# First weight sums of the second feed-forward made ahead in the first output stage, with a reordered opening, convolution statistics and last gate

## The chip, the cores and the metric

The kernel runs on one core of a Trainium2 chip. The metric is device time in microseconds (us). The engines are PE (TensorE, matmuls and transposes), DVE (VectorE), ACT (ScalarE), POOL (GpSimd) and SP (SyncE, which only issues transfers). Each has a queue of its own and works through it in order; an instruction at its head that waits holds up what is queued behind it.

## The reference

One encoder layer over 1024 tokens of width 1024, in float32, with three residual sub-layers, cut to its core:

```
x = post_norm(x, mod0, 0.5, h -> (silu(h@w1[:, :2816]) * (h@w1[:, 2816:])) @ w1_out)
x = post_norm(x, mod1, 1.0, h -> concat(conformer_conv(h), diff_attention(h)) @ mix_w_out)
x = post_norm(x, mod2, 0.5, h -> (silu(h@w2[:, :2816]) * (h@w2[:, 2816:])) @ w2_out)
post_norm(x, (shift, scale, gate), w, f) =
    layer_norm(2**0.25 * x + w * (1 + gate) * f(x * (1 + scale) + shift)) * g + b
mod = (silu(c) @ w_ada + b_ada), nine rows of 1024
```

## The kernel before, in words

**Stages.** In order of time: the opening, which makes shift and scale of the first sub-layer; the first feed-forward's input phase (to about 495 us); its output stage (to 711); the mixer's projections and convolution (to about 900); attention (to 1125); the mixer's output product (to 1224); the start of the second feed-forward, here called the middle (to about 1300); its input phase (to 1660) and its output stage (to the end).

**Products.** The feed-forward matrices are multiplied by a scheme of seven block products in place of eight, so sums of blocks of weights (`sf`, `S1` to `S4`) and of activations (`r_kt`, `T1` to `T4`) are made first. Every float32 operand is then split into a high part (a copy on ACT, names that end in h) and a low part (a subtraction on DVE or POOL, names in l), and each block product is three matmuls: high by high, high by low, low by high. In the input phase a step j handles 128 gate and 128 up columns; `ra_j`, `rb_j` (or `r_j`, `r4`) are its raw weights, `ah`/`al` the split gate blocks, `sh`/`sl` the split sums, `fi_j` its results in PSUM. In the output stage 77 steps (`prep`, then 12 matmuls `fo`) run over seven products n and 11 blocks k; `prep` runs four steps ahead (`AHEAD`) and makes `gl` and `wr`. `evac` empties the products.

**Opening.** For each of four column blocks kk, `first_mod` forms a row-vector product: DVE sums six of eight weight rows into `ada0a`, PE adds up over partitions (`ada0p`) and does the other two rows itself (`ada0q`); ACT then makes the columns A and B and from them `h`, whose split is `r_kkbh`, `r_kkbl`.

**Attention.** While heads are worked on, the convolution's channel statistics run as side work: `conv_stat(half)` makes `cv` and `cr` on POOL, waits `ST` = 5 turns of the loop and makes `cnm` on DVE. POOL also does the differential subtraction `p`, which is 2.4 us each.

**Middle.** The string `MSEQ` is an order written by hand: tokens for the last pieces of the mixer's output (m, d), the transposes of the normalised x (f, F), the splits and sums of activations (r, s, t, u, v, b), gate splits (G), the weight sums of j = 0 and 1 (X, x, Y, y), raw weights and sums of j = 2 (W) and product steps (p). The letters V and G behind a token name DVE or POOL. An exclamation mark lets the token be issued only behind the last PE piece.

**Last gate.** `ada_gate` makes the last sub-layer's gate row in two halves: eight weight rows are loaded in four pieces `adaw` of 512 KB and summed on DVE (`ada`, L155 and L157), then PE and DVE finish it.

Spill and weight transfers go over SP's queue, the output pieces `gd`, `mwo`, `spill` and `mwi` over POOL's.

Of the kernel before, what the change touches and what calls it, by code (L numbers as in the profile page):

```python
# [38 lines left out]
MSEQ = "m5 G0 f0 r0V f1 d5 r1G !m6 f2 r2V f3 d6 r3G m7 d7 F0 !X0GV x0V | !Y0VG p01 p02 s0GV y0V F2 G1 t0V F1 s1VV t1G s2VV p11 !F3 !X1GV s3VV b0 t2V t3V u0GV b1 v0V u1GG v1V b2 b3 !p12 Y1GG u3VV u2GV v2V v3V x1V !p06 y1G p05 !p16 !p07 p15 !p03 !p17 p04 W0 p13 !p14"  # L39
# [11 lines left out]
def layer_kernel(ctx, tc, a, out):  # L51
# [483 lines left out]
    def out_phase(s, wp, w_out, gd, gate, xs, done, after):  # L535
# [13 lines left out]
        def prep(n, k):  # L549
# [144 lines left out]
    mwi = [dram.tile([D, 2, H], F32, name=f"mwi{g}", tag="mwi", bufs=3) for g in range(3)]  # L694
    mwo = [dram.tile([P, 2, 2, H], F32, name=f"mwo{j}", tag="mwo", bufs=8) for j in range(8)]
    with pool("p1a") as wp:
# [464 lines left out]
    with pool("mattn") as wp:  # L1161
# [81 lines left out]
        def conv_stat(half):  # L1243
# [70 lines left out]
    with pool("p3a") as wp:  # L1314
# [70 lines left out]
        def token(st, tok, n3):  # L1385
# [29 lines left out]
            elif c in "XY":  # L1415
# [141 lines left out]
```

## Time and profile before

| | |
|---|---|
| Runs | 1895.30, 1894.91, 1892.62 us; median 1894.91 |
| Profiled execution | 1899.15 us, its span 1897.4 us |
| Mean granted TensorE clock | 0.99 of full speed |
| PE busy | 1826.3 us |
| DVE busy | 1439.1 us |
| ACT busy | 784.9 us |
| POOL busy | 317.4 us |

The profiled execution lies 4.24 us above the median of the runs. Its time is 1.75 us above its span. Busy time of a matmul includes its drain, so back-to-back matmuls of 128x512 that are shown at 0.39 us start 0.2275 us apart; at half the clock the same ones are shown at 0.63 us.

### The profile page before, as it was taken

To read this page: it belongs to the slowest core of one execution; us is meant where nothing else is said; L and a number is where in the kernel's file an instruction comes from. 1 tells how busy PE (TensorE), PEld (TensorE's weight loads), DVE (VectorE), ACT (ScalarE), POOL (GpSimd) and SP (SyncE) were. 2 spreads that over 40 slices of the span, in tenths; PEclk is the share of its full clock that TensorE was granted. 3 is DMA by queue.
4 is the path that set the end of the run, shared out by engine and by line. 5 is a ranking of instruction groups with operands and counts; after the bars stand their busy time and mean duration, and the time that the engine had idled before them with its cause. 6 is when DMAs were issued, how large, how long until landed. Compare 5 with 4: busy or idle time off the path is not lost. (4 is left out here: it accounts for less than half of the span.)

```text
span 1897.4 us, 23451 instructions
## 1 busy us (share of the span) xinstructions
PE 1826.3 (96%) x8570; PEld 1513.1 (80%) x8570; DVE 1439.1 (76%) x1979; ACT 784.9 (41%) x1292; POOL 317.4 (17%) x322
## 2 busy tenths in 40 slices
PE   5999999999999999999999899979999999999997
PEld 5787888887888887887888788758887888888885
DVE  4988877897688777999676566587776665469888
ACT  2643333333445543122277781453332333354540
POOL 0001111011200011036467540350000000000011
PEclk9999999999999999999999999989999999999999
DMA  9268867785894323222000134125554433187432
GB/s 319 72 225 281 257 228 239 242 268 189 301 322 131 100 60 134 83 95 70 20 1 1 45 134 134 78 83 183 167 166 152 145 120 106 45 293 275 135 113 72
DMA packets 219378, 288.73 MB, mean 152 GB/s; under 512 B 15978, under 2 KB 126687, under 8 KB 219262
## 3 DMA queue, kind: packets, MB, share of 16 engines
q1 hardware_dynamic: 204842, 245.25, 39.9%
q0 software_dynamic: 11072, 38.80, 5.6%
q10 hardware_dynamic: 3348, 3.18, 0.5%
q8 instruction: 67, 1.10, 0.2%
q14 instruction: 49, 0.40, 0.1%
HBM read 209.06 MB, written 78.12 MB: 151 GB/s over the span
## 5 line engine op out<-in xcount | busy, mean ns | idle before, releaser
L587 PE MATMUL fo<-wr,gl 128*128 128x512 f32 x1848 | 421.5, 390 | 1.0 <-DVE pv L630 1.0
L587 PEld LDWEIGHTS fo<-wr,gl 128*128 128x128 f32 x1848 | 346.3, 188 | 74.1 <-DVE pv L630 1.4
L1000 DVE SCALAR_TENSOR_TENSOR cacc<-u,convw,cacc 128x1012 f32<-128x1012 f32 (+14 forms) x120 | 150.9, 1322 | 0.2
L144 DVE TENSOR_TENSOR gl<-gr,gl 128x512 fp32r<-128x512 f32 x148 | 101.4, 691 | 12.5 <-ACT gl L143 11.0
L143 ACT CAST gl<-gr 128x512 fp32r<-128x512 f32 x148 | 90.8, 618 | 26.3 <-DMA gr<-gd 19.4
L144 DVE TENSOR_TENSOR sl<-sf,sh 128x1024 fp32r<-128x1024 f32 x43 | 54.5, 1267 | 59.0 <-ACT sh L143 58.9
L1131 DVE TENSOR_REDUCE mx<-sc 128x1 f32<-128x1024 f32 x64 | 75.5, 1215 | 26.2 <-PE sc L1129 26.0
L219 POOL TENSOR_TENSOR rr<-rv,mhalf 128x1 f32<-128x1 f32 x24 | 22.2, 925 | 431.4 <-DVE rv L217 431.4
L157 DVE SCALAR_TENSOR_TENSOR ada<-adaw,c_act,ada 128x512 f32<-128x512 f32 x98 | 73.2, 747 | 25.3 <-DMA adaw<-in_w_ada_dram 24.8
L143 ACT CAST sh<-sf 128x1024 fp32r<-128x1024 f32 x44 | 46.4, 1054 | 104.8 <-PE fi_16S L373 5.8
L1133 ACT ACTIVATE p<-sc,mx 128x1024 f32<-128x1024 f32 x64 | 71.4, 1117 | 36.1 <-DVE mx L1131 36.0
L395 POOL DMA_DIRECT2D gd<-gf x8 | 4.4, 546 | 413.6 <-DVE gf L461 412.5
L423 ACT ACTIVATE gf<-gf 128x512 f32<-128x512 f32 x44 | 27.8, 632 | 106.0 <-DVE gf L422 103.0
L143 ACT CAST wr<-wa 128x512 fp32r<-128x512 f32 x66 | 41.2, 624 | 71.1 <-PE fo L587 70.1
L443 ACT ACTIVATE gf<-gf 128x512 f32<-128x512 f32 x44 | 27.7, 629 | 98.8 <-DVE gf L442 98.8
L981 PE MATMUL glu<-hm,gluh 128*128 128x512 f32 x256 | 65.6, 392 | 0.0
L1182 POOL TENSOR_TENSOR p<-p,p 128x1024 f32<-128x1024 f32 x27 | 64.2, 2377 | 1.5
L143 ACT CAST wr<-wb 128x512 fp32r<-128x512 f32 x66 | 40.2, 621 | 57.5 <-PE fo L587 40.4
L144 DVE TENSOR_TENSOR wr<-wa,wr 128x512 fp32r<-128x512 f32 x66 | 45.4, 687 | 24.0 <-ACT wr L143 23.7
L1199 PE MATMUL av<-vf,aT 128*128 128x128 f32 x512 | 62.4, 276 | 1.0 <-ACT cacc L1262 1.0
L144 DVE TENSOR_TENSOR sl<-r,sh 128x1024 fp32r<-128x1024 f32 x44 | 53.6, 1221 | 11.8 <-ACT sh L143 11.7
L1199 PEld LDWEIGHTS av<-vf,aT 128*128 128x128 f32 x512 | 59.7, 192 | 1.5 <-ACT cacc L1262 1.3
(3436 smaller groups left out, 4874.1 us busy)
## 6 DMA issues: line engine op xcount, KB each, us to landing
gr<-gd SPq DMA_DIRECT2D x148, 256.0 KB
adaw<-in_w_ada_dram SPq DMA_DIRECT2D x56, 512.0 KB
gd<-gf SPq DMA_DIRECT2D x102, 256.0 KB
r<-in_ffn_w_in_dram SPq DMA_DIRECT2D x84, 256.0 KB
ra<-in_ffn_w_in_dram SPq DMA_DIRECT2D x66, 256.0 KB
mwi<-mw POOLq DMA_DIRECT2D x24, 512.0 KB, 5.9
wb<-in_ffn_w_out_dram SPq DMA_DIRECT2D x44, 256.0 KB
wa<-in_ffn_w_out_dram SPq DMA_DIRECT2D x44, 256.0 KB
```

What stands on the lines that cost most here:

```text
L143: a = S.copy(hi, x)
L144: b = eng.tensor_tensor(lo, x, hi.bitcast(F32), ALU.subtract)
L157: V.scalar_tensor_tensor(acc, raw[:, jj], c_act[:, n : n + 1], acc, ALU.mult, ALU.add)
L423: S.activation(c0, c0, AF.Silu)
L443: pace["S"] = S.activation(c1, c1, AF.Silu).ins
L587: PE.matmul(ps, lhsT=g[:, x, ts_], rhs=w[:, y], start=n in (1, 2, 3) and k == i == 0, stop=k == NK - 1 and i == 2, skip_group_check=n not ...
L981: PE.matmul(q[2 * m + h], lhsT=w[:, m * P : (m + 1) * P], rhs=hm[k][h][:, x], start=k == 0 and n == 0, stop=k == KD - 1 and n == 2,)
L1000: V.scalar_tensor_tensor(acc[:, lo_t:hi_t], u[:, lo_t + sh : hi_t + sh], convw[:, i, jj : jj + 1], acc[:, lo_t:hi_t], ALU.mult, ALU.add,)
L1131: V.tensor_reduce(mx_, ps, axis=AX.X, op=ALU.max, negate=True)
L1133: S.activation(pe, ps, AF.Exp, bias=mx_, accum_out=sm[:, e : e + 1])
L1182: last = G.tensor_tensor(p0, p0, p1, ALU.add)
L1199: PE.matmul(ps[:, 0:P], lhsT=aT[:, kt], rhs=vf[kt][:, h * P : (h + 1) * P], start=kt == 0, stop=kt == 7)
```

## The change

Five places change.

1. **Opening.** DVE sums seven of the eight weight rows and PE one (`NV` now counts rows). The high split `r_kbh` is put right behind `h` of the same block and the next block's columns are ordered behind it (`rounded`); the gate split of j = 0 and its weight sums are put at blocks 0, 1 and 3.
2. **First output stage.** During steps 0 to 71 the sums S1 to S4 of the second feed-forward's weights of j = 0 and j = 1 are made, in eight pieces (a piece is one of two j by one of four k). Every nine steps POOL's queue loads a piece (`sums_load`), and six steps later DVE and ACT make its four sums with their split (`sums_part`), which POOL's queue stores to two new DRAM tiles `mws`.
3. **Attention.** `conv_stat` waits 10 turns in place of 5.
4. **Middle.** The tokens X, x, Y, y are gone; S and T load the ready sums by eight SP transfers of 512 KB. r1, r3 and t1 change from G to V.
5. **Last gate.** `ada_gate` has a staged form: two pieces are loaded and four rows summed, one step later the other two, then the rest, driven from `hook2` at j = 10 to 17; the second half begins at 14 in place of 13.

```diff
-MSEQ = "m5 G0 f0 r0V f1 d5 r1G !m6 f2 r2V f3 d6 r3G m7 d7 F0 !X0GV x0V | !Y0VG p01 p02 s0GV y0V F2 G1 t0V F1 s1VV t1G s2VV p11 !F3 !X1GV s3VV b0 t2V t3V u0GV b1 v0V u1GG v1V b2 b3 !p12 Y1GG u3VV u2GV v2V v3V x1V !p06 y1G p05 !p16 !p07 p15 !p03 !p17 p04 W0 p13 !p14"
+MSEQ = "m5 G0 f0 r0V f1 d5 r1V !m6 f2 r2V f3 S0 d6 r3V m7 d7 F0 | p01 p02 s0VV F2 G1 t0V F1 s1VV t1V s2VV p11 !F3 T0 S1 s3VV b0 t2V t3V u0GV b1 v0V u1GG v1V b2 b3 !p12 u3VV u2GV v2V v3V !p06 p05 T1 !p16 !p07 p15 !p03 !p17 p04 W0 p13 !p14"
-NV = (3, 3, 3, 3)
+NV = (7, 7, 7, 7)
...
+            with tc.issue_after(pace["Y"]):
+                fetch(0)
+                fetch(1)
+            yield
+            for n in (0, 2):
+                with tc.issue_after(pace["V"]):
+                    for q in (n, n + 1):
+                        ada_acc([raws[q]], acc, 2 * q)
+                if n == 0:
+                    with tc.issue_after(pace["Y"]):
+                        fetch(2)
+                        fetch(3)
+                    yield
+            yield
+            rest(acc)
...
+        w2 = a["ffn2_w_in"][0].rearrange("(k e p) (s n) -> k e p s n", e=2, p=P, s=2)
+
+        def sums_load(j, k):
+
+            t = wp.tile([P, 2, 4, P], F32, tag="ms", bufs=1, name=f"ms{j}{k}")
+            for e in range(2):
+                G.dma_start(t[:, 0, 1:3] if e else t[:, 0, 0::3], w2[k, e][:, :, j * P : (j + 1) * P])
+            return t
+
+        def sums_part(t, j, k):
+
+            r = t[:, 0]
+            with tc.issue_after(pace["V"]), tc.issue_after(pace["S"]):
+                V.tensor_tensor(r[:, 2], r[:, 3], r[:, 2], ALU.add)
+                V.tensor_tensor(r[:, 3], r[:, 0], r[:, 3], ALU.subtract)
+                V.tensor_tensor(r[:, 0], r[:, 2], r[:, 0], ALU.subtract)
+                V.tensor_tensor(r[:, 1], r[:, 1], r[:, 0], ALU.subtract)
+                S.copy(t[:, 1].bitcast(F32R), r)
+                V.tensor_tensor(r.bitcast(F32R), r, t[:, 1], ALU.subtract)
+            for x in range(2):
+                G.dma_start(mws[j][:, x, :, k], t[:, x])
...
+            if s == 0 and i < 72:
+                if i % 9 == 2:
+                    ms = sums_load(i // 36, i // 9 % 4)
+                elif i % 9 == 8:
+                    sums_part(ms, i // 36, i // 9 % 4)
...
-            for j in range(2 * n):
+            for j in range(n):
...
-                with tc.issue_after(columns) if kk else nullcontext():
+                with ExitStack() as es:
+                    if kk:
+                        es.enter_context(tc.issue_after(columns))
+                        es.enter_context(tc.issue_after(rounded))
                     summed, columns = first_mod(kk, ada[kk], NV[kk])
                     hb.append(first_h(kk, xb[kk], 0))
+                    hi.append(slot(f"r0_{kk}bh"))
+                    rounded = S.copy(hi[kk], hb[kk]).ins
                 with tc.issue_after(summed):
                     if kk:
-                        right_first(f"r0_{kk - 1}", ops, hb[kk - 1])
-                    if kk == 1:
+                        right_lo(kk - 1)
+                    if kk == 0:
                         L[0].update(in_gate(wp, s, 0, raws[0]))
-                    if kk == 3:
-                        right_first("r0_3", ops, hb[3])
-                        in_sums(wp, s, 0, raws[0], L[0])
+                    elif kk == 1:
+                        in_sums(wp, s, 0, raws[0], L[0], order=(0,))
+                    elif kk == 3:
+                        right_lo(3)
+                        in_sums(wp, s, 0, raws[0], L[0], order=(1,))
...
-            for _ in range(ST):
+            for _ in range(2 * ST):
                 yield
...
+            elif c in "ST":
+                i = int(c == "T")
+                parts = []
+                for x, tag in ((1, "sh"), (0, "sl")):
+                    parts.append(wp.tile([P, 2, 4, P], F32R, tag=tag, bufs=3, name=f"{tag}2_{k}_{i}"))
+                    SY.dma_start(parts[-1].bitcast(F32), mws[k][:, x, i::2])
...
-            if j in (10, 13):
+            if j in (10, 14):
...
-            if j in todo2:
-                todo2.pop(j)()
+            if 10 <= j <= 17:
+                next(todo2["gate"], None)
```

Three places show what the orders become. The first is DVE's queue in the opening, from the second block's split on; `ada0a` are the row sums (x2 counts two in a row), `al_0` the low part of j = 0's gate blocks, `r_kbl` the low part of block k of h. Before:

```order
L729 TENSOR_SCALAR ada0a_317<-ada_1_0_219,c_act 128x512
L731 SCALAR_TENSOR_TENSOR ada0a_317<-ada_1_0_219,c_act,ada0a_317 128x512
L731 SCALAR_TENSOR_TENSOR ada0a_317<-ada_1_1_222,c_act,ada0a_317 128x512 x2
L731 SCALAR_TENSOR_TENSOR ada0a_317<-ada_1_2_225,c_act,ada0a_317 128x512 x2
L144 TENSOR_TENSOR al_0_363<-r_0_200,ah_0_362 128x1536
L144 TENSOR_TENSOR r_0bl<-h_0_0_313,r_0bh 128x1024
L729 TENSOR_SCALAR ada0a_367<-ada_2_0_233,c_act 128x512
L731 SCALAR_TENSOR_TENSOR ada0a_367<-ada_2_0_233,c_act,ada0a_367 128x512
L731 SCALAR_TENSOR_TENSOR ada0a_367<-ada_2_1_236,c_act,ada0a_367 128x512 x2
L731 SCALAR_TENSOR_TENSOR ada0a_367<-ada_2_2_239,c_act,ada0a_367 128x512 x2
L144 TENSOR_TENSOR r_1bl<-h_1_0_355,r_1bh 128x1024
L729 TENSOR_SCALAR ada0a_413<-ada_3_0_247,c_act 128x512
```

After:

```order
L144 TENSOR_TENSOR al_0_318<-r_0_202,ah_0_317 128x1536
L782 TENSOR_SCALAR ada0a_322<-ada_1_0_221,c_act 128x512
L784 SCALAR_TENSOR_TENSOR ada0a_322<-ada_1_0_221,c_act,ada0a_322 128x512
L784 SCALAR_TENSOR_TENSOR ada0a_322<-ada_1_1_224,c_act,ada0a_322 128x512 x2
L784 SCALAR_TENSOR_TENSOR ada0a_322<-ada_1_2_227,c_act,ada0a_322 128x512 x2
L784 SCALAR_TENSOR_TENSOR ada0a_322<-ada_1_3_230,c_act,ada0a_322 128x512
L366 TENSOR_TENSOR r_0_202<-r_0_202 128x512
L367 TENSOR_TENSOR r_0_202<-r_0_202 128x512
L368 TENSOR_TENSOR r_0_202<-r_0_202 128x512
L834 TENSOR_TENSOR r_0bl<-h_0_0_312,r_0bh 128x1024
L144 TENSOR_TENSOR sl_0_0_368<-r_0_202,sh_0_0_367 128x1024
L782 TENSOR_SCALAR ada0a_372<-ada_2_0_235,c_act 128x512
```

The gate's low part stands ahead of the second block's sums, three weight sums and `sl_0_0` stand between the second and third blocks, and each block has one more row.

The second place is POOL's queue in the middle, where the last two tiles of the mixer's output are normalised; `rr_k` is the reciprocal deviation of tile k, `spill_k` its store, `sf_2` the sums of j = 2. Before:

```order
L144 TENSOR_TENSOR r_1bl<-h_10279,r_1bh 128x1024
L1420 TENSOR_TENSOR sf_0_0_10434<-rb_0_9871,ra_0_9870 128x512
L219 TENSOR_TENSOR rr_6_10371<-rv_6_10369,mhalf 128x1
L1327 DMA spill_6_9660<-x_6_9697 128x1024
L144 TENSOR_TENSOR r_3bl<-h_10352,r_3bh 128x1024
L219 TENSOR_TENSOR rr_7_10416<-rv_7_10414,mhalf 128x1
L1424 TENSOR_TENSOR sf_0_1_10518<-ra_0_9870,sf_0_0_10434 128x512
L1327 DMA spill_7_9661<-x_7_9699 128x1024
L1403 TENSOR_TENSOR r_0t_10552<-h_10422,h_10263 128x512
L1420 TENSOR_TENSOR sf_1_0_10629<-rb_1_9877,ra_1_9876 128x512
L1409 TENSOR_TENSOR h_10422<-h_10422 128x512
L1409 TENSOR_TENSOR h_10579<-h_10579 128x512
```

After:

```order
L244 TENSOR_TENSOR rr_5_10376<-rv_5_10374,mhalf 128x1
L1394 DMA spill_5_9737<-x_5_9773 128x1024
L373 TENSOR_TENSOR sf_2_0_10893<-rb_2_10884,ra_2_10883 128x512
L375 TENSOR_TENSOR sf_2_1_10894<-ra_2_10883,rb_2_10884 128x512
L374 TENSOR_TENSOR sf_2_0_10893<-sf_2_0_10893,ra_2_10883 128x512
L244 TENSOR_TENSOR rr_6_10453<-rv_6_10451,mhalf 128x1
L376 TENSOR_TENSOR sf_2_1_10894<-ra_2_10883,sf_2_0_10893 128x512
L1394 DMA spill_6_9738<-x_6_9775 128x1024
L244 TENSOR_TENSOR rr_7_10498<-rv_7_10496,mhalf 128x1
L1394 DMA spill_7_9739<-x_7_9777 128x1024
L1476 TENSOR_TENSOR h_10504<-h_10504 128x512
L1476 TENSOR_TENSOR h_10647<-h_10647 128x512
```

POOL loses the splits `r_1bl`, `r_3bl`, `r_1t1l`, and the sums of j = 0 and 1; the sums of j = 2 stand ahead of and behind `rr_6`.

The third place is DVE's queue in attention at the second half's statistics; `mx` are the row maxima of the scores. Before:

```order
L1237 BN_STATS cst_9092<-cT_9087 128x6
L1238 BN_AGGR cmv_8871<-cst_9092 128x2
L1252 SCALAR_TENSOR_TENSOR cnm_9232<-cmv_8871,cr_9167 128x4
L1131 TENSOR_REDUCE mx_9127<-sc_9122 128x1
L1131 TENSOR_REDUCE mx_9136<-sc_9131 128x1
L1191 COPY aT_9140<-aT_9147 128x512
```

After:

```order
L1304 BN_STATS cst_9160<-cT_9155 128x6
L1305 BN_AGGR cmv_8949<-cst_9160 128x2
L1198 TENSOR_REDUCE mx_9195<-sc_9190 128x1
L1198 TENSOR_REDUCE mx_9204<-sc_9199 128x1
L1319 SCALAR_TENSOR_TENSOR cnm_9416<-cmv_8949,cr_9308 128x4
L1258 COPY aT_9208<-aT_9215 128x512
```

`cnm` stands behind the two maxima; the first half's `cnm` keeps its place.

## Rows read from the trace of the kernel before

**Rows 1.** The page's first part: busy time, share and instructions of each engine.

```profile
PE 1826.3 (96%) x8570; PEld 1513.1 (80%) x8570; DVE 1439.1 (76%) x1979; ACT 784.9 (41%) x1292; POOL 317.4 (17%) x322
```

**Rows 2.** Windows by stage: busy us (instructions) of PE, PEld, DVE, ACT, POOL; clock; DMA.

```profile
0.00:100.00 100.00, 75.48 (x332) 63.84 (x333) 68.03 (x90) 47.64 (x85) 2.01 (x9) 1.00 0.65 198
...
495.00:711.00 216.00, 215.85 (x968) 178.12 (x967) 176.03 (x294) 107.78 (x178) 16.84 (x21) 1.00 0.54 176
...
1224.00:1300.00 76.00, 63.45 (x257) 48.72 (x257) 64.98 (x65) 38.01 (x49) 30.26 (x19) 0.89 0.34 111
```

**Rows 3.** Timeline of DVE in the opening: start, us, instruction, idle before.

```profile
32.04 1.23 DVE L144 TENSOR_TENSOR r_0bl<-h,r_0bh 128x1024 fp32r<-128x1024 f32 x1 [7.36 <-ACT r_0bh L143]
...
42.64 1.23 DVE L144 TENSOR_TENSOR r_1bl<-h,r_1bh 128x1024 fp32r<-128x1024 f32 x1 [5.04 <-ACT r_1bh L143]
...
44.30 3.90 DVE L731 SCALAR_TENSOR_TENSOR ada0a<-ada,c_act,ada0a 128x512 f32<-128x512 f32 x5
...
57.78 1.29 DVE L811 TENSOR_TENSOR t<-h,h 128x512 f32<-128x512 f32 x2
```

**Rows 4.** Waits of PE, 0 to 100 us: total, times, longest.

```profile
PE ada0q L737 <- DMA ada<-in_w_ada_dram: 12.1, 2, 10.3
PE ada0p L747 <- DVE ada0a L731: 6.1, 2, 3.5
```

**Rows 5.** First output stage: DVE and PE timeline, one window, ACT's waits to 600.

```profile
574.13 0.67 DVE L144 TENSOR_TENSOR wr<-wa,wr 128x512 fp32r<-128x512 f32 x1
496.42 179.89 PE L587 MATMUL fo<-wr,gl 128*128 128x512 f32 x792
555.00:565.00 10.00, 10.00 (x46) 8.29 (x45) 10.00 (x17) 3.81 (x7) 0.00 (x0) 1.00 0.91 290
ACT wr L143 <- PE fo L587: 31.1, 21, 1.6
```

**Rows 6.** Attention around the second half's statistics: timelines of POOL and PE, DVE's wait.

```profile
1082.63 2.38 POOL L1182 TENSOR_TENSOR p<-p,p 128x1024 f32<-128x1024 f32 x1
1085.38 1.02 POOL L1248 TENSOR_TENSOR cr<-cv,mhalf 128x4 f32<-128x4 f32 x1
DVE cnm L1252 <- POOL cr L1248: 8.7, 2, 4.4
1089.52 0.71 PE L1113 MATMUL qTl<-ident_r,ql 128*128 128x128 f32 x4 [2.49 <-DVE aT L1191]
```

**Rows 7.** Windows in attention, the middle and behind the gate, columns as above.

```profile
1090.00:1100.00 10.00, 10.00 (x62) 8.89 (x62) 6.28 (x9) 9.18 (x22) 6.75 (x4) 0.85 0.05 16
...
1250.00:1260.00 10.00, 5.15 (x14) 3.05 (x13) 10.00 (x8) 3.15 (x4) 6.34 (x4) 0.67 0.37 105
...
1440.00:1450.00 10.00, 10.00 (x37) 8.08 (x38) 8.81 (x12) 2.70 (x3) 0.00 (x0) 0.83 0.49 167
```

**Rows 8.** Timelines of PE, DVE and POOL in the middle.

```profile
1229.14 0.50 PE L373 MATMUL fi_0A<-r_3bl,ah 128*128 128x512 f32 x1 [1.93 <-POOL r_3bl L144]
1240.19 1.09 PE L1335 MATMUL hT<-ident,x 128*128 128x128 f32 x8 [0.61 <-ACT h L255]
1245.88 2.83 DVE L1403 TENSOR_TENSOR r_2t<-h,h 128x512 f32<-128x512 f32 x1
1244.89 3.27 POOL L144 TENSOR_TENSOR r_1t1l<-r_1t,r_1t1h 128x1024 fp32r<-128x1024 f32 x1
1248.21 0.50 PE L373 MATMUL fi_0A<-r_1t1l,sh 128*128 128x512 f32 x1 [2.85 <-POOL r_1t1l L144]
1287.59 0.39 PE L373 MATMUL fi_2A<-r_0bh,ah 128*128 128x512 f32 x1
```

**Rows 9.** DMA traffic from 1215 to 1262 in 40 slices.

```profile
GB/s 164 282 0 0 0 0 0 0 251 195 0 0 0 0 0 47 275 349 330 303 49 0 0 0 7 0 0 0 0 0 91 133 231 304 134 0 0 0 0 0
```

**Rows 10.** The gate's first half: DVE timeline, and PE's wait, 1420 to 1470.

```profile
1433.78 1.54 DVE L157 SCALAR_TENSOR_TENSOR ada<-adaw,c_act,ada 128x512 f32<-128x512 f32 x2 [3.52 <-DMA adaw<-in_w_ada_dram]
PE fi_9A L373 <- DVE p L439: 2.4, 1, 2.4
```

More of the change, by code (lines that the diff above doesn't have):

```diff
@@ L2 @@
-from contextlib import nullcontext
+from contextlib import ExitStack
 import concourse.bass as bass
@@ L148, in layer_kernel, with ada_acc @@
     w_ada = a["w_ada"][0].rearrange("(p j) n -> p j n", j=KD)
-    def ada_acc(raws, acc):
-        n = 0
+    def ada_acc(raws, acc, n=0):
         for raw in raws:
@@ L185, in ada_cols, with ada_gate, slow, fetch @@
         return rest
-    def ada_gate(wp, take, s, w, g, half):
+    def ada_gate(wp, take, s, w, g, half, staged=False):
         if half == 0:
             SY.dma_start(g, a["b_ada"][:, (s * 3 + 2) * D : (s * 3 + 3) * D].partition_broadcast(P))
-        acc = ada_chunk(wp, take, s, 2, half)
-        def rest():
+        def slow():
+            col = (s * 3 + 2) * D + half * H
+            acc = wp.tile([P, H], F32, tag="ada_acc", bufs=1, name=f"ada{s}2{half}")
+            raws = {}
+            def fetch(q):
+                raws[q] = take(f"adaw{s}2{half}{q}")
+                SY.dma_start(raws[q], w_ada[:, 2 * q : 2 * q + 2, col : col + H])
+            with tc.issue_after(pace["Y"]):
[13 more added lines that the diff above has]
+            rest(acc)
+        acc0 = None if staged else ada_chunk(wp, take, s, 2, half)
+        def rest(acc=acc0):
             ps = bank(f"adag{s}{half}")
@@ L197, in rest @@
             V.scalar_tensor_tensor(sl, ps, w, sl, ALU.mult, ALU.add)
-        return rest
+        return slow() if staged else rest
     def raw_slot(name):
@@ L576, in prep @@
                 right[n, k] = wp.tile([P, 2, H], F32R, tag="wo", bufs=WO + 2 * (s == 2), name=name)
-            split(right[n, k][:, 0], right[n, k][:, 1], src)
+            pace["S"], pace["V"] = split(right[n, k][:, 0], right[n, k][:, 1], src)
             if n == 1:
@@ L694, in layer_kernel @@
     mwi = [dram.tile([D, 2, H], F32, name=f"mwi{g}", tag="mwi", bufs=3) for g in range(3)]
+    mws = [dram.tile([P, 2, 4, 4, P], F32, name=f"mws{j}", tag="mws", bufs=2) for j in range(2)]
     mwo = [dram.tile([P, 2, 2, H], F32, name=f"mwo{j}", tag="mwo", bufs=8) for j in range(8)]
@@ L735, in first_mod @@
                 m, es, k = i // 2, slice(i % 2 * P, (i % 2 + 1) * P), 2 * kk + i % 2
-                for j in range(2 * n, KD):
+                for j in range(n, KD):
                     PE.matmul(
                         two[:, i : i + 1], lhsT=raws[j // 2][:, j % 2, m, es], rhs=c_act[:, j : j + 1],
-                        start=j == 2 * n, stop=j == KD - 1,
+                        start=j == n, stop=j == KD - 1,
                     )
@@ L1349, in layer_kernel @@
         left = [{}, {}]
-        sums, t12 = {}, {}
+        t12 = {}
         def mout(c, t):
@@ L1379, in play @@
                 if tok[0] == "!":
-                    with tc.issue_after((lastn if tok[1] in "XY" else pe_last)[-1]):
+                    with tc.issue_after(pe_last[-1]):
                         token(st, tok[1:], n3)
@@ L1414, in token @@
                 left[k].update(in_gate(wp, 2, k, raws[k]))
[L1415 to L1429 removed]
+            elif c in "ST":
[4 more added lines that the diff above has]
+                    SY.dma_start(parts[-1].bitcast(F32), mws[k][:, x, i::2])
                 for n in range(2):
[L1431 removed]
+                    left[k][f"S{2 * i + 2 - n}"] = (parts[0][:, n], parts[1][:, n])
             elif c == "p":
@@ L1477, in hook2 @@
                 with tc.issue_after(pace["Y"]):
-                    todo2[j + 2] = ada_gate(wp, raw_slot, 2, 0.5, mods["gate2"], (j - 10) // 3)
-            if j in todo2:
-                todo2.pop(j)()
+                    todo2["gate"] = ada_gate(wp, raw_slot, 2, 0.5, mods["gate2"], (j - 10) // 4, staged=True)
+            if 10 <= j <= 17:
+                next(todo2["gate"], None)
         def early2(wp, s, w_in, ops):
```

21 lines of the change are left out of this document (6 added, 15 removed).

## The prediction

> **What bounds the kernel now.** I read the page's busy shares first: PE is busy for 1826.3 us, DVE for 1439.1 [rows 1], against a span of 1897.4. So PE bounds the kernel, and a change can shorten it only where PE stands idle (71 us in all) or runs at a lower clock. The windows by stage then say where that is: 24.5 us in the first 100, 12.55 in the middle from 1224 to 1300, and 0.15 in the whole first output stage [rows 2]. The windows of 10 us show the clock: it is at 1.00 (2.4 GHz) nearly everywhere, and a mean of 0.85, 0.67 or 0.83 where PE had just waited, so part of such a stretch ran at 1.2 GHz [rows 7]. A wait therefore costs its own length and something behind it. Last I read the waits and the timelines around each place that the diff touches; what they show is given with each part.
>
> **The opening.** DVE's low splits wait 7.36 and 5.04 us for the high half that ACT makes [rows 3]: r_0bh stands on ACT behind the next block's h, which needs the next block's columns, for which DVE's own sums are needed. From one low split to the next, at 32.04 and 42.64, pass 10.6 us, of which DVE works some 5.6. PE waits 6.1 us for these sums [rows 4]. After the change r_kbh comes a block earlier, so a round on DVE is one row longer (3.90 us for five rows, 0.78 each) and has no such wait: 0.5 + 6 x 0.78 + 1.23 = 6.4 us. Going through DVE's new order: the second block's sums end at about 24, three weight sums of 0.7 follow to 26.2, r_0bl to 27.4, sl_0_0 waits for a copy that ACT can make after the second h, to about 32; the sums of blocks 2 and 3 and r_1bl end at 43.4. The last sums end at 48.2 before (44.30 + 3.90), so 4.8 us are gained; the first t starts at 57.78 before [rows 3] and some 6 us earlier by the same count. DVE has no gap of note for some time behind it, and PE follows it. I take **-5.5**. The bound below is -3: PE's other wait here, 12.1 us, is for the weights themselves [rows 4], and the last of them cannot come earlier; the bound above is -9, if PE's 6.1 and the 2 to 3 us of gaps behind it all go.
>
> **The pieces in the first output stage.** Eight pieces, each of four subtractions of 128x128, one copy of 128x512 on ACT and one subtraction of 128x512 on DVE. The trace has no 128x128 subtraction; it lies between nothing and the 0.67 us of 128x512 [rows 5]. I take 0.25, a little over its quarter, so DVE has 4 x 0.25 + 0.7 = 1.7 us a piece, 13.6 in all (at most 3.4 and 27). What hides it: PE runs 66 steps in 179.89 us, 2.726 each, without a gap [rows 5]. The low half of the right operand of step 31 (the 32nd of 77 such rows) ends on DVE at 574.8, and PE takes it up at 496.42 + 31 x 2.726 = 580.9, so DVE is 6.1 us ahead. The same count gives 5.7 us at the least from 545 to 583, and 6.9 or more behind. That stretch is the tight one: DVE is busy 10.00 of 10 us [rows 5], so what the pieces of steps 17 and 26 (about 543 and 567) take there is not won back before about 577: 5.7 - 3.4 leaves 2.3 us. Behind it DVE has gaps again. That ACT waits 31.1 us for wr buffers until 600 [rows 5] says the same: the preparation is held by PE, not PE by it. The loads and stores (four a piece, 32 in all) stand in POOL's queue, which is busy 16.84 of 216 us [rows 2]; behind them stand the rr of the finished tiles, for which the next stage has time, and at 690 one hm, 20 us ahead of its use. I take **0**, bounds 0 and +6. If the cover were gone, it would cost the 13.6 us.
>
> **Attention.** DVE waits 8.7 us for cr in two waits, the longest 4.4: one for each half's cnm. The second half's cr stands on POOL behind a p of 2.38 us; behind cnm on DVE stand the maxima and the copy aT, for which PE waits 2.49 us [rows 6]. The 10 us behind it run at 0.85, which costs 1.5 us [rows 7]. After the change cnm stands behind the two maxima, which take 2.35 us together and end when cr is nearly there; aT then waits some 1.1 us, which PE's own work ahead of it covers. The first half's cnm keeps its place in DVE's queue although the diff changes both: its wait stays. I take **-3.5** of 4.0, bounds -1 (the remaining wait still lowers the clock) and -5.
>
> **The middle.** Of 76 us PE is busy 63.45 at a clock of 0.89 [rows 2]: 12.55 us of waits and 7 to 8 of clock, about 20 lost. The waits name POOL's splits (r_3bl 1.93, r_1t1l 2.85) and DVE's [rows 8]. DVE's same subtraction of 128x512, 0.67 us alone [rows 5], takes 2.83 while POOL works on r_1t1l [rows 8]: POOL's 30.26 us in this stage [rows 2] slow DVE. After the change POOL keeps four subtractions of h and, ahead of them, the four sums of j = 2; the splits that PE waited for go to DVE, and DVE and ACT lose the sums and splits of j = 0 and 1. What remains is late elsewhere. POOL now has j = 2's sums ahead of rr_6; I count the last tile some 1.5 us later than now, and PE idle 4 us around 1227 to 1233, where 1.93 show now [rows 8], with 1.5 us of clock. The transfers of T0 and S1 are issued only behind the last transposes, at 1240.19 [rows 8]; four of 512 KB at the 349 GB/s that the fullest slice shows [rows 9] take 6 us, so S1 lands at about 1248, where PE wants it at 1246: 2 to 3 us with its clock. So of 20 lost, 7 remain and **-13** are gained. The bounds are -18 (only 2 remain) and -6 (the waits for rr_6, for the loads and their clock take two thirds). The Trainium skill ("GPSIMD Engine Reference", section 8, Key points) says that GpSimd shares its SBUF interfaces with VectorE and contends with DVE instructions that have two SBUF inputs. The 2.83 us show that here; by this rule j = 2's sums and the h that POOL keeps would go on stretching DVE, and by the 2.83 against 0.67 six us of POOL would cost DVE some 4, a gain of 9 in place of 13. The bounds hold that too.
>
> **The last gate.** DVE waits 3.52 us at its head for adaw; behind the rows stands p, for which PE waits 2.4 us [rows 10], and the 10 us from 1440 run at 0.83, 1.7 us [rows 7]. Staged, the rows are summed three and more steps behind their loads, and the wait has no cause. The second half has the same wait and no stall of PE, so it gives nothing. **-4**, bounds -2 and -4.5.
>
> **The sum.** -5.5 + 0 - 3.5 - 13 - 4 = -26. Against the profiled execution's own 1899.15 that is 1873.1; the median of the runs lies 4.24 lower, so 1868.9, rounded to **1869**. All ends that favour it give -36.5 (1858), all against it -6 (1889).
>
> **The rivals.** *The middle's waits only change their names* (0.20). The order in which POOL now makes j = 2's sums ahead of rr_6, and loads that begin at 1240, speak for it; that DVE has 16 us less to do speaks against. The gain there is 6: -19, 1876.
> *The opening is bound by its transfers* (0.13). For: PE's longest wait, 12.1 us in two, is for them [rows 4]. Against: the later blocks' waits name DVE. The opening gives 1: -21.5, 1873.
> *Waits take the place of most of those removed* (0.06): rr_6, the loads and the stretched DVE cost what the middle gains, the opening gains nothing; -3 to 0, 1893.
> *The pieces make DVE the bound of the first output stage* (0.09), the case on the other side. A piece's load waits until both stores of the piece before have landed, since there is one buffer; DVE's first subtraction waits for the load, and the wr of four steps stand behind it. DVE is 5.7 us ahead, so PE loses nothing until the pieces hold DVE up by that much in the full stretch; to eat the 26 us the eight must hold it up by 32, 4 each. At 5 each PE loses 34: +8, 1903. For it speaks a DMA share of 0.91 there [rows 5]; against, that a period is 24.5 us long and the load has 16 of them.
>
> **How the numbers follow.** The forecast has 0.52, the rivals 0.20, 0.13, 0.06 and 0.09. This kernel's measurement can tell 0.2%, 3.8 us. Faster by more than that are the forecast and the first two rivals, 0.85; within it the third, 0.06; slower 0.09. The range runs from 1857 to 1889: the sum's two ends, which hold the first two rivals; the last two, 0.15, lie outside.
>
> **What would show it.** In the opening: no wait of DVE for r_kbh over 2 us in blocks 2 and 3, and the first t at about 52. In the first output stage: PE's idle time under 1 us, and DVE's some 14 us more busy; a wait of fo for wr of steps 28 to 37 would show the rival. In attention: the second cnm waits about 1 us and PE no longer 2.49 behind it; the first keeps its 4.4. In the middle: first fi_2A some 48 to 52 us behind the start of the stage, not 63.6 (1287.59 from 1224 [rows 8]); DVE's subtractions at 0.67; a wait of PE for x_7 or rr_6 at the start, and for sh of j = 1. At the gate: no wait of fi_9A for p, and the clock at 1.00 behind it. The forecast is wrong if the first output stage shows waits of PE, or if the middle keeps its 12 us of idle time.

## The result, and the profile after

| | before | after |
|---|---|---|
| Median of the runs | 1894.88 us (4 runs, 1892.62 to 1895.30) | 1873.27 us (4 runs, 1872.60 to 1874.93) |
| Ratio to before | 1 | 0.989, 95% interval 0.9873 to 0.9907 |
| Profiled execution, its span | 1899.15, 1897.4 | 1873.36, 1871.6 |

The time fell by 21.6 us in the medians and by 25.8 us between the two profiled executions. The prediction was 1869 with a range of 1857 to 1889.

The line of the page after that answers to [rows 1]: PE shows 18 us less as busy, DVE, ACT and POOL about the same.

```profile
PE 1808.2 (97%) x8538; PEld 1499.2 (80%) x8538; DVE 1438.0 (77%) x2021; ACT 785.0 (42%) x1296; POOL 320.7 (17%) x344
```

Where the time went is read from the starts of PE's first instructions of each stage, in the two timelines. The lines show two of the stages, the first output stage (before, it starts at 496.42 [rows 5]) and the middle, each time before and then after.

```profile
710.41 0.47 PE L981 MATMUL glu<-hm,gluh 128*128 128x512 f32 x1
489.89 177.16 PE L612 MATMUL fo<-wr,gl 128*128 128x512 f32 x780
707.59 0.47 PE L1048 MATMUL glu<-hm,gluh 128*128 128x512 f32 x1
...
1224.05 0.39 PE L1363 MATMUL mo<-moh,fl 128*128 128x512 f32 x1
1421.10 0.39 PE L373 MATMUL fi_9A<-r_0bh,ah 128*128 128x512 f32 x1
1216.21 0.39 PE L1430 MATMUL mo<-moh,fl 128*128 128x512 f32 x1
1399.71 0.39 PE L398 MATMUL fi_9A<-r_0bh,ah 128*128 128x512 f32 x1
```

Lengths in us:

| Stage, from and to | before | after | change | predicted |
|---|---|---|---|---|
| opening, to the first fi_2A | 99.4 | 93.5 | -5.9 | -5.5 |
| first input phase, to the first fo | 397.0 | 396.4 | -0.6 | 0 |
| first output stage, to the first glu | 214.0 | 217.7 | +3.7 | 0 |
| projections, to the first score | 226.1 | 224.5 | -1.6 | 0 |
| attention, to the first mo | 196.6 | 193.1 | -3.5 | -3.5 |
| mixer's output, to the last mo | 91.0 | 91.0 | 0.0 | 0 |
| middle, to the first fi_9A | 197.1 | 183.5 | -13.6 | -13 |
| gate, to the first fi_11A | 42.4 | 38.1 | -4.3 | -4 |
| the rest, to the end of PE's last fo | 422.4 | 422.3 | -0.1 | 0 |

The windows after, with the columns of [rows 2], at the places that answer to its rows (the stages begin earlier now): the first output stage has 2.9 us of idle PE where there were 0.15 (the rest of its 3.7 us lies in PE's busy time, which includes the drain), and the middle 5.3 where there were 12.55, at a clock of 1.00 in place of 0.89, with POOL busy for 9.33 us in place of 30.26.

```profile
0.00:100.00 100.00, 74.54 (x326) 62.58 (x327) 76.77 (x101) 49.91 (x87) 2.00 (x9) 1.00 0.66 203
490.00:708.00 218.00, 215.07 (x961) 176.69 (x959) 184.12 (x333) 111.36 (x185) 38.26 (x53) 1.00 0.60 201
1216.00:1292.00 76.00, 70.72 (x316) 55.64 (x315) 59.96 (x73) 38.95 (x50) 9.33 (x8) 1.00 0.45 153
1430.00:1440.00 10.00, 10.00 (x46) 8.29 (x45) 7.62 (x11) 4.20 (x5) 0.00 (x0) 1.00 0.09 26
```

**The opening.** DVE's timeline, to be set beside [rows 3]. The fourth block's sums now end at 44.0 (48.2 before), and the first t starts 5.5 us earlier. One wait has moved and not gone: r_3bl waits 4.24 us, since the last columns need the last sums, whatever the order. This stage is not the same in every execution: it takes 92.4 to 93.7 us in the ten profiles with the new opening and 99.1 to 99.4 in the four with the old one, so the gain lies between 5.4 and 7.0 us.

```profile
33.04 4.69 DVE L784 SCALAR_TENSOR_TENSOR ada0a<-ada,c_act,ada0a 128x512 f32<-128x512 f32 x6
37.64 1.22 DVE L834 TENSOR_TENSOR r_1bl<-h,r_1bh 128x1024 fp32r<-128x1024 f32 x1
...
39.30 4.69 DVE L784 SCALAR_TENSOR_TENSOR ada0a<-ada,c_act,ada0a 128x512 f32<-128x512 f32 x6
...
49.96 1.23 DVE L834 TENSOR_TENSOR r_3bl<-h,r_3bh 128x1024 fp32r<-128x1024 f32 x1 [4.24 <-ACT r_3bh L847]
...
52.24 0.68 DVE L878 TENSOR_TENSOR t<-h,h 128x512 f32<-128x512 f32 x1
```

**The first output stage.** PE's waits after from 485 to 715, then one chain of them in the timelines of POOL, DVE, ACT and PE. The reciprocal rr stands on POOL behind the store of a piece's low half. It is late, so DVE waits 2.83 us at nm. The normalisation on ACT (L260) waits for nm, and ACT's copies for wr stand behind it; on DVE the evacuation pv stands behind nm and behind the wr that needs those copies. PE waits for pv.

```profile
PE fo L612 <- DVE pv L655: 1.5, 1, 1.5
PE fo L612 <- DVE wr L144: 0.9, 1, 0.9
PE fo L612 <- ACT wr L143: 0.5, 1, 0.5
```

```profile
660.13 0.79 POOL L688 DMA_DIRECT2D mws<-ms  x1 [3.61 <-ACT ms L685]
660.18 0.68 DVE L686 TENSOR_TENSOR ms<-ms 128x512 fp32r<-128x512 f32 x1
...
663.21 0.76 POOL L688 DMA_DIRECT2D mws<-ms  x1 [2.30 <-issue]
663.99 0.57 POOL L244 TENSOR_TENSOR rr<-rv,mhalf 128x1 f32<-128x1 f32 x1
664.59 0.21 DVE L259 TENSOR_SCALAR nm<-mv,rr 128x1 f32<-128x1 f32 x1 [2.83 <-POOL rr L244]
664.84 1.25 ACT L260 ACTIVATE x<-x,nm,rr 128x1024 f32<-128x1024 f32 x1 [4.60 <-DVE nm L259]
...
666.62 1.29 DVE L144 TENSOR_TENSOR wr<-wb,wr 128x512 fp32r<-128x512 f32 x2 [1.82 <-ACT wr L143]
667.84 0.69 DVE L655 TENSOR_TENSOR pv<-fo,pv 128x512 f32<-128x512 f32 x1
668.58 3.05 PE L612 MATMUL fo<-wr,gl 128*128 128x512 f32 x12 [1.52 <-DVE pv L655]
```

What the second store waits for is not its data: the low half (L686) is ready at 660.86, and the store starts 2.35 us later. The profile names no wait there ("issue"). But the piece's first store, issued at 660.13, takes some 2.8 us to land (the line, of the DMA view from 655 to 672), and the trace has its landing at 662.88. In all eight pieces the second store starts 0.33 us behind the landing of the first, 3.0 to 6.7 us behind the first one's own start, with its data ready before. Why POOL's queue holds it until then is not shown; the two loads of a piece, of 128 KB each, go out there one right behind the other, in 1.47 us.

```profile
mws<-ms POOLq DMA_DIRECT2D x2, 256.0 KB, 2.8
```

**Attention.** DVE's two cnm, beside [rows 6]. The first waits 4.36 us as before; the second waits 1.08, behind the maxima.

```profile
1053.22 0.16 DVE L1319 SCALAR_TENSOR_TENSOR cnm<-cmv,cr 128x4 f32<-128x4 f32 x1 [4.36 <-POOL cr L1315]
...
1081.86 0.17 DVE L1319 SCALAR_TENSOR_TENSOR cnm<-cmv,cr 128x4 f32<-128x4 f32 x1 [1.08 <-POOL cr L1315]
```

**The middle.** Its waits and its transfers, beside [rows 8] and [rows 9]: PE's longest wait is now 1.82 us for the last tile (L260 is its normalisation). No wait of PE names a transfer. The first fi_2A starts 50.2 us behind the start of the stage, inside the 48 to 52 that the prediction named. DVE's r_2bl takes 2.18 us while POOL makes the last of the sums of j = 2, where r_3bl takes 1.23 with POOL idle.

```profile
1220.49 0.50 PE L398 MATMUL fi_0A<-r_3bl,ah 128*128 128x512 f32 x1 [0.76 <-DVE r_3bl L144]
1224.42 0.77 PE L1402 MATMUL hT<-ident,x 128*128 128x128 f32 x5 [1.82 <-ACT x L260]
1238.45 0.47 PE L398 MATMUL fi_1S<-r_0t1h,sh 128*128 128x512 f32 x1 [1.02 <-DVE r_3t L1470]
...
1215.40 2.18 DVE L144 TENSOR_TENSOR r_2bl<-h,r_2bh 128x1024 fp32r<-128x1024 f32 x1
...
1219.21 1.23 DVE L144 TENSOR_TENSOR r_3bl<-h,r_3bh 128x1024 fp32r<-128x1024 f32 x1 [0.30 <-ACT r_3bh L143]
```

The DMA view from 1215 to 1262 in 40 slices: the four loads behind the last transposes are the block that begins at 1232.6, and it is over by 1239.

```profile
GB/s 333 34 108 338 0 0 0 0 0 303 143 0 0 0 0 167 375 392 387 384 94 0 0 0 0 157 366 359 10 0 0 0 87 324 268 185 28 0 0 104
```

**The gate.** From 1395 to 1530 no wait of PE is left (2.4 us before, [rows 10]), and the window from 1430 runs at 1.00.

### The profile page after: what moved, and what is told of

Read it like the earlier page. It is cut to its first block, busy times and chain, and to the rows that moved or that the text cites. A ratio compares the mean times of both kernels' runs of the same rounds, so it can differ in the third digit from the quotient of the medians.

```text
span 1871.6 us, 23505 instructions
## 1 busy us (share of the span) xinstructions
PE 1808.2 (97%) x8538; PEld 1499.2 (80%) x8538; DVE 1438.0 (77%) x2021; ACT 785.0 (42%) x1296; POOL 320.7 (17%) x344
## 4 chain that ended last, share of the span: by engine, by line
PE 74%; DVE 11%; POOL 4%; DMA 4%; ACT 4%; issue 3%; POOLq 0%; SPq 0%; DVEq 0%; ACTq 0%
PE fo L612 17%; PE glu L1048 4%; PE mo L1430 4%; PE vp L1095 2%; PE kp L1095 2%; ACT p L1200 2%; PE fi_13A L398 1%; PE fi_9A L398 1%; PE fi_14A L398 1%; PE fi_6A L398 1%; PE fi_4A L398 1%; PE fi_10A L398 1%; PE fi_21A L398 1%; PE fi_11A L398 1%; PE fi_16A L398 1%
## 5 line engine op out<-in xcount | busy, mean ns | idle before, releaser
L612 PE MATMUL fo<-wr,gl 128*128 128x512 f32 x1848 | 422.3, 390 | 3.9 <-DVE pv L655 2.5
L144 DVE TENSOR_TENSOR sl<-sf,sh 128x1024 fp32r<-128x1024 f32 x40 | 49.0, 1225 | 69.3 <-ACT sh L143 69.2
L143 ACT CAST sh<-sf 128x1024 fp32r<-128x1024 f32 x40 | 42.1, 1053 | 106.5 <-issue 12.1
```

The source lines that it names most:

```text
L143: a = S.copy(hi, x)
L144: b = eng.tensor_tensor(lo, x, hi.bitcast(F32), ALU.subtract)
L612: PE.matmul(ps, lhsT=g[:, x, ts_], rhs=w[:, y], start=n in (1, 2, 3) and k == i == 0, stop=k == NK - 1 and i == 2, skip_group_check=n not ...
```

## The experiments

All are judged by two things: the median of the runs, and the lengths of the stages in their profiles, counted as in the table above. The second is the finer measure here. The runs of the kernel before spread from 1892.26 to 1902.64 over three jobs, each on a chip of its own, while a stage that an edit doesn't touch mostly came out the same within 0.3 us. The exceptions are the opening (above), the first output stage with SP's stores (below), and what is told at the end. The changed kernel itself ran in none of these jobs, and each ratio is against the kernel before in the same job. By these ratios alone, attention undone, the gate undone, the splits on POOL and a piece in seven steps can't be told from the changed kernel (0.9873 to 0.9907); what is said of them rests on the stages of one profile each.

**Opening undone.** The functions `first_mod` and `early` and `NV` as before, all else changed.

```diff
-NV = (7, 7, 7, 7)
+NV = (3, 3, 3, 3)
...
```

> The changed kernel with the opening of before (six rows on DVE, the old order of splits and sums), all else as changed. Theory (each part is worth what its own stretch shows in the two profiles): the first matmul of the first output stage comes 6.5 us later again, the time is 1873.3 + 6.5 = 1879.8. Rival (the transfers bind the opening, or the gain is eaten by a later wait): 1873 to 1875.

Measured 1881.13 us, ratio to before 0.9923 (0.9909 to 0.9937). The opening took 99.1 us (93.5 in the changed kernel), so 5.6 us come back there and nothing behind it takes them up. The median is 7.9 above the changed kernel's; attention was 1.4 us and the projections 1.5 us longer in this profile, by the clock (below).

**Attention undone.**

```diff
-            for _ in range(2 * ST):
+            for _ in range(ST):
```

> The changed kernel with 5 turns in conv_stat again. Theory: only the second half's cnm moved, so its 4.36 us wait on DVE and PE's 2.5 us come back with a clock of about 0.85 behind them: + 3.5, 1876.8. Rival (the stretch from the convolution to attention's end gained 5 us, all by this edit): + 5, 1878.3. Rival (the side work is hidden anyway): 1873.3.

Measured 1876.06 us, 0.9894 (0.9878 to 0.991). Attention took 196.5 us in place of 193.1: 3.4 us. Both waits of DVE for cr are back, and behind each the clock falls; the lines are DVE's waits from 1030 to 1130 and two windows.

```profile
DVE cnm L1319 <- POOL cr L1315: 8.7, 2, 4.4
```

```profile
1050.00:1060.00 10.00, 7.06 (x41) 5.95 (x40) 5.79 (x10) 7.56 (x15) 4.76 (x5) 0.83 0.15 52
1080.00:1090.00 10.00, 7.52 (x47) 6.64 (x47) 6.77 (x11) 9.19 (x18) 3.71 (x3) 0.83 0.32 105
```

**Gate undone.** `hook2` as before, so `ada_gate` is not staged.

```diff
...
-            if 10 <= j <= 17:
-                next(todo2["gate"], None)
+            if j in todo2:
+                todo2.pop(j)()
```

> The changed kernel with the last gate unstaged, as before. Theory: DVE's wait of 3.5 us for the gate's weights and PE's 2.4 us wait for p come back, with a clock of 0.83 behind: + 4.4, 1877.7. Rival (the place has moved and the weights now land in time): 1873.3.

Measured 1876.40 us, 0.9897 (0.988 to 0.9913). The stage took 39.3 us in place of 38.1, and the phase behind it 0.4 more: 1.7 us and not 4.4. DVE's wait for the weights is back at nearly its length, but PE waits only 1.0 us for p, and the clock does not fall. The lines are PE's wait from 1395 to 1530, DVE's timeline and the window.

```profile
PE fi_9A L398 <- DVE p L464: 1.0, 1, 1.0
```

```profile
1412.10 1.54 DVE L156 SCALAR_TENSOR_TENSOR ada<-adaw,c_act,ada 128x512 f32<-128x512 f32 x2 [3.02 <-DMA adaw<-in_w_ada_dram]
```

```profile
1415.00:1425.00 10.00, 9.04 (x41) 7.15 (x40) 9.95 (x13) 3.75 (x4) 0.00 (x0) 1.00 0.34 119
```

So the edits overlap. With the old middle, the unstaged gate's stage takes 41.9 to 42.9 us in three profiles, and staging saves 4.3 (38.1 in the next experiment). With the new middle, the stage takes 39.3 unstaged, so some 3 of the 4.3 us come with either change: the wait of PE is 1.4 us shorter and the clock does not fall. DVE is further ahead there: its first row of the gate starts 4.5 us behind the first fi_9A (5.4 before), and the weights that it then waits for are issued at 6.0 (6.9 before). The kernels with the old middle and an unstaged gate also lack the edits of the opening and of attention; that it is the middle that gives this lead is argued, not shown.

**Pieces and their use undone.** The kernel before with the changes to the opening, attention and the gate only: no `sums_load`, `sums_part` or `mws`, and the old `MSEQ`.

> The changed kernel without the eight pieces and with the middle's old order of tokens; opening, attention and gate as changed. Theory: the middle's 13.5 us are lost again and the 3.7 us that the first output stage lost come back: + 9.8, 1883.1. Rival (the pieces cost nothing and the 3.7 us have another cause): + 13.5, 1886.8, with the waits of fo for pv and wr still there. Rival (the middle gains because the whole program runs earlier, not by its order): under + 5.

Measured 1881.95 us, 0.9927 (0.9912 to 0.9941). The first output stage took 214.0 us as before, with no wait for pv or wr; the middle 196.6. So pieces and middle together are worth 13.1 - 3.7 = 9.4 us, as the theory has it. That the whole program runs earlier is not the cause: here it does, and the middle is as long as before.

**The pieces alone**, added to the kernel before; nothing reads `mws`.

> The kernel before with the eight pieces and their stores added and nothing reading them. Theory: + 3.7 us against the kernel before, 1898.6, all of it in steps 60 to 75 of the first output stage, where reciprocals and mask products of POOL stand behind stores. Rival (DVE's 13.6 us of added work are the price, in the full stretch from 545 to 583): PE waits there, at steps 18 to 32.

Measured 1900.57 us, 1.0014 (1.0002 to 1.0026). The stage took 217.8 us, and its waits are those of the changed kernel. PE waits nowhere from 545 to 583. So the price of 3.8 us is the pieces' own and falls at the stage's end.

```profile
PE fo L587 <- DVE pv L630: 1.6, 1, 1.6
PE fo L587 <- DVE wr L144: 0.9, 1, 0.9
...
PE fo L587 <- ACT wr L143: 0.5, 1, 0.5
```

**Stores on SP's queue.**

```diff
-                G.dma_start(mws[j][:, x, :, k], t[:, x])
+                SY.dma_start(mws[j][:, x, :, k], t[:, x])
```

> The changed kernel with the pieces' stores issued by SP's queue in place of POOL's; loads and sums unchanged. Theory (rr and hm on POOL stand behind stores that wait for the piece's low half, and DVE waits for rr and hm): PE's 2.9 us of waits in the first output stage fall below 1, 1873.3 - 3 = 1870.3. Rival (the price is DVE's and ACT's own work): 1873.3, with the same waits. Second rival (SP's queue now waits for the low half and the weight loads come late): slower, above 1875.

Measured 1871.12 us, 0.9861 (0.9848 to 0.9873). The stage took 215.3 us: 2.4 of the 3.7 are gone, with the same work on DVE and ACT. PE no longer waits for pv, and the longest wait of DVE for an rr falls from 2.83 to 0.7. So POOL's queue is the cause of these, though not as the theory has it: there the second store waited for the landing of the first, and on SP's queue it follows 0.7 to 1.3 us behind the first. The 1.3 that stay are waits for wr behind the last piece's work. The second rival came in part: ACT's waits for the transfers gr, which SP's queue issues, rise from 12.3 to 33.4 us in the stage, and PE loses nothing by that in this profile. Lines: PE's waits from 485 to 722, DVE's from 620.

```profile
PE fo L612 <- ACT wr L143: 0.5, 1, 0.5
PE fo L612 <- DVE wr L144: 0.4, 1, 0.4
...
DVE nm L259 <- POOL rr L244: 3.9, 7, 0.7
```

**A piece in seven steps.**

```diff
-            if s == 0 and i < 72:
-                if i % 9 == 2:
-                    ms = sums_load(i // 36, i // 9 % 4)
-                elif i % 9 == 8:
-                    sums_part(ms, i // 36, i // 9 % 4)
+            if s == 0 and i < 56:
+                if i % 7 == 0:
+                    ms = sums_load(i // 28, i // 7 % 4)
+                elif i % 7 == 6:
+                    sums_part(ms, i // 28, i // 7 % 4)
```

> The changed kernel with one piece in seven steps in place of nine (load at the first, sums at the seventh), so that all sums are made by step 55, ahead of most of the normalisation of finished tiles. Theory (POOL's order): no wait of PE for pv or wr at the end of the stage, 1873.3 - 3 = 1870.3. Rival (DVE's own work in its full stretch): four pieces in place of three stand before step 32, DVE's lead of 5.7 us shrinks by another 1.7 and PE waits at steps 28 to 45: above 1874.

Measured 1879.36 us, 0.9904 (0.989 to 0.9917). The rival was right: the stage took 221.9 us. The waits at its end are gone, but PE waits at step 32, where DVE's lead is used up, and at step 44, where ACT's copies pu are late behind a piece's copy and a gl whose transfer is late (PE's timeline). Around step 44 the granted clock is 0.95 and 0.87 in the two windows of 10 us from 605 to 625.

```profile
577.95 3.02 PE L612 MATMUL fo<-wr,gl 128*128 128x512 f32 x12 [1.75 <-DVE wr L144]
...
614.62 61.93 PE L612 MATMUL fo<-wr,gl 128*128 128x512 f32 x266 [3.69 <-ACT pu L631]
```

**Both cnm behind the latest maximum.**

```diff
-                V.tensor_reduce(mx_, ps, axis=AX.X, op=ALU.max, negate=True)
+                pace["mx"] = V.tensor_reduce(mx_, ps, axis=AX.X, op=ALU.max, negate=True).ins
...
-            V.scalar_tensor_tensor(nm, mv[:, :, 0], -1.0, r, ALU.mult, ALU.mult)
+            with tc.issue_after(pace["mx"]):
+                V.scalar_tensor_tensor(nm, mv[:, :, 0], -1.0, r, ALU.mult, ALU.mult)
```

> The changed kernel with both halves' cnm ordered behind the latest score maximum at the place of the program where it is written. Theory (the first half's cnm kept its place, and its 4.36 us on DVE cost PE 2.3 us and some clock): - 3.5, 1869.8. Rival (behind both is the transposed convolution and its norms, which then come late): no gain or + 1.

Measured 1868.97 us, 0.9851 (0.9839 to 0.9864). Attention took 189.5 us, 3.6 less than in the changed kernel: the first half's wait was worth as much as the second's. No cnm waits any more; PE's longest wait in the stretch is 1.2 us.

**The splits of the middle on POOL again.** In `MSEQ`, `r1V`, `r3V` and `t1V` become `r1G`, `r3G` and `t1G`; the sums still come ready.

> The changed kernel with r1, r3 and t1 of the middle left to POOL as before; the sums still come ready from DRAM. Theory (the middle's 13.6 us come from both: POOL's splits that PE waited for, and POOL's work that stretched DVE): about half is lost again, + 4 to + 7, 1877 to 1880, with PE waiting for r_3bl and r_1t1l on POOL. Rival (the sums alone were the load): under + 2, 1875.

Measured 1876.17 us, 0.9879 (0.9865 to 0.9892). The middle took 186.1 us, 2.6 more, below the theory's range and above the rival's. Of the 13.6 us 2.6 come from the three splits and, by difference, some 11 from the sums. PE waits for two of the splits by name (1210 to 1290), and the clock falls in the window of the first.

```profile
PE fi_0A L398 <- POOL r_3bl L144: 2.4, 1, 2.4
...
PE fi_0A L398 <- POOL r_1t1l L144: 1.3, 1, 1.3
```

```profile
1220.00:1230.00 10.00, 7.59 (x23) 5.34 (x22) 3.95 (x9) 3.75 (x5) 5.97 (x6) 0.66 0.26 105
```

**Both mends together**, SP's stores and both cnm.

> The changed kernel with the stores of the pieces on SP's queue and both halves' cnm behind the latest maximum. Theory: the two gains add up, 2.5 in the first output stage and 3.6 in attention: 1873.3 - 6.1 = 1867.2. Rival (the gain of one is eaten by waits behind it): 1869 to 1871.

Measured 1867.75 us, 0.9831 (0.9818 to 0.9845): faster than the changed kernel (0.9873 to 0.9907); the two intervals, each against the runs of before in its own job, do not touch. Attention took 189.5 us; the first output stage 216.5, with a new wait of 1.1 us for pu at step 44, so only 1.2 of the 2.4 stay here. This stage's code is the same as with SP's stores alone, where it took 215.3 without that wait, so its price of 1.3 to 2.5 us changes from one execution to another. The pu stand on ACT behind a gl that waits 1.60 us for a transfer gr of SP's queue.

**Both mends, a piece in eight steps**: `i < 64`, loads at `i % 8 == 0`, sums at 5.

> As the kernel with both mends, with a piece in eight steps (load at the first, sums at the sixth), the last sums at step 61 in place of 71. Theory (what is left of the first output stage's price, 1.3 us, is the last piece's own load in front of the wr of steps 70 and 71): the stage takes 214.0 us as in the kernel before, 1866. Rival (the lead of DVE in its full stretch up to step 45 is used up, as with a piece in seven steps): the stage takes over 216, 1868 and more.

Measured 1869.33 us, 0.9845 (0.9832 to 0.9858). The wr waits are gone, and the one for pu is 2.0 us, with a clock of 0.92 and 0.91 around it in the two windows from 605 to 625 (1.00 with a piece in nine steps): 217.7 us. The stage came out as the rival has it: an earlier last piece moved the price to the middle of the stage. It is one profile each, 1.2 us apart, no more than the two profiles of equal code above; the intervals of the two kernels overlap.

**The kernel before once more**, unchanged.

> The kernel before once more, unchanged, for a second profile. Theory (the profiled execution before lay 4.2 us above the median of three runs by the spread of the runs alone): stages of the same lengths within 0.3 us, but for the first input phase, which took 395 to 399 us in eight kernels of equal code there, and the two places where a wait of equal length did or did not lower the clock. Rival (that profile has a loss of its own that the others lack): one stage shorter by 3 us and more.

Measured 1896.80 us (one run; span 1895.0). Opening 99.3, first output stage 214.0, mixer's output 91.0: the same. Shorter are the first input phase by 0.9, the projections by 1.6 and the middle by 1.4 us; attention and the gate's stage are 0.8 and 0.5 longer. So no one stage of the first profile has a loss of its own of 3 us. The 1.6 us of the projections are a wait of equal length with another clock: the windows of the two profiles, first the one before. All fourteen profiles bear this out: PE is busy for 28.5 to 28.6 of the 30 us from 855 to 885 in each, the granted clock there is 0.94 in the seven in which the projections take 226.0 or 226.1 us, and 1.00 in the seven in which they take 224.5 or 224.6.

```profile
860.00:880.00 20.00, 18.53 (x84) 14.96 (x83) 20.00 (x19) 6.25 (x17) 5.50 (x4) 0.91 0.00 1
```

```profile
860.00:880.00 20.00, 18.58 (x92) 15.17 (x91) 20.00 (x18) 5.32 (x14) 7.10 (x3) 1.00 0.00 1
```

## Why the prediction came out as it did

The mechanism was right in four of five parts, and the sum met the two profiles: -26 forecast, -25.8 measured. That they meet so closely is luck: the first output stage cost 3.7 us that were not in the sum, and the projections gave 1.6 and the other stages some 2 more than forecast. One step behind the sum failed as well.

- **Opening, -5.5.** Measured -5.9, and 5.6 when undone (5.4 to 7.0 over all profiles). The count through DVE's new order was right to a microsecond (last sums at 43.4 forecast, 44.0; first t about 52, 52.24). The sign named for it, no wait for r_kbh over 2 us, was wrong for the last block (4.24). What the transfers bind, PE's wait for ada, rose from 12.1 to 14.8 us; the rival that rested on it did not come.
- **First output stage, 0.** Measured +3.7: the term was mis-sized, inside its bounds of 0 and +6. The step that failed is "behind them stand the rr of the finished tiles, for which the next stage has time". The next stage has, but DVE does not: nm waits for rr at the head of DVE's queue, with the evacuation and wr behind it. The prediction read POOL's share of busy time (16.84 of 216 us) as room, and did not count how long a store there holds up what is behind it. 1.2 to 2.4 us go when the stores leave POOL's queue. Waits of PE here were the prediction's own sign that it is wrong. The cover in the full stretch (5.7 us of lead, two pieces of 1.7) held as counted, as the piece in seven steps showed from the other side: one piece more there, and PE waits. A subtraction of 128x128 took 0.28 to 0.29 us where 0.25 were taken, and the pieces' operations on DVE 15 us in all; its busy time in the windows rose by 8.1 only, since the ends of operations overlap and count once.
- **Attention, -3.5.** Measured -3.5, and 3.4 when undone. The second cnm waits 1.08 us (forecast 1.1) and the first keeps its 4.36. The price of the first, left in place, is 3.6.
- **Middle, -13.** Measured -13.6, 13.1 when undone, and 12.2 against the second profile of the kernel before. What remained was forecast as 7 us: measured, PE idles 5.3 us in the windows and loses nothing to the clock. From the start of the stage to the first fi_2A, DVE is busy for 39.8 us in place of 55.1; the prediction had 16 less. The wait for the last tile came (1.82 for hT). The loads of T0 and S1 did not hold PE up; they moved at up to 392 GB/s, and DVE's r chain was the later one. POOL's remaining work still stretches DVE: 2.18 against 1.23 us for r_2bl and r_3bl. The Trainium skill ("GPSIMD Engine Reference", section 8, Key points) states such contention for instructions with two SBUF inputs, and the trace agrees. But it fell on operations that PE hardly waited for, and the gain of 9 that the prediction worked out for that case did not come.
- **Gate, -4.** The stage gave -4.3, but undoing the edit gives back 1.7 only. The step was right for the edit on the old kernel; beside the other edits, some 2.6 of it come anyway. The parts of the sum were counted as if they were independent.
- **What was not forecast** are the 1.6 us of the projections, which no edit touches; the second profile of the kernel before has them too. They are the clock's.
- **The median.** 1873.27 lies 4.4 above 1869. The step that failed is the last one, that the median lies 4.24 below the profiled execution after the change as well: the changed kernel's profiled execution, 1873.36, lies at its median. The runs of the kernel before spread by 10 us, and in later jobs its medians were 1895.71, 1897.46 and 1899.55, so the three runs shown were low ones, or their chip a faster one; which is open. Of the spread, the clock after equal waits is one cause that the profiles show. The first input phase is another place: it took 395.3 to 398.9 us in fourteen profiles of equal code there, the three with SP's stores the longest (398.0 to 398.9). Why is open.

Of the rivals, none came. The one on the other side named the right place and the wrong point: it looked at DVE's lead and the loads, and most of the price came by POOL's queue.

## What to carry to other kernels

An engine that is idle for most of the time is still a queue in order: ask what small operation stands there behind a transfer, how long the queue holds that transfer back (here until the store ahead of it had landed), and which busy engine waits for that operation at the head of its own queue. Work placed under cover needs its slack counted at every step, since the stage that is tight in the middle and the one that is tight at the end forbid each other's mends. Terms of a sum can overlap, as the gate's did with the other edits; undo each alone to see it, and compare the lengths of stages, not whole times, where the runs spread more than the effect.

## What the hardware showed unexpectedly

Waits of equal length did and did not lower the clock: 1.5 us of idle PE in the window from 860 to 880 left it at 0.91 or at 1.00 in two profiles of one kernel, and the stage was 1.6 us longer or shorter by that, seven times each in fourteen profiles. With waits of 2.3 to 2.5 us in attention, windows of 10 us at or behind them show between 0.68 and 0.88, and attention took 193.1 or 194.5 us with a longest wait of 2.3 or 2.4.

On POOL's queue the second of two stores of 256 KB, with its data ready, started 0.33 us behind the landing of the first in all eight pieces, and in the chain shown above a reciprocal waited behind it. On SP's queue the same store started 0.7 to 1.3 us behind the first.
